# 192 unused bytes per partition among the constants of a transformer layer

## The chip, the cores and the metric

The kernel is one program on 1 core of a Trainium2 chip. The metric is the device time of one execution in microseconds, median of several runs. Every number below is of the kernel before the change.

## The reference

One layer, batch 1, 1024 positions, model width 1024, all in float32:

```python
x = x + 0.5 * swiglu(rms_norm(x, g_ffn1), w1_gate, w1_up, w1_down)      # d_ff 2816
h = rms_norm(x, g_mix);  proj = h @ w_in                                # 10 slices
y_a = dsa_attention(...)             # indexer scores, top 256 keys of each query, 8 heads of 64
y_b = stick_breaking_attention(...)  # 8 heads of 64, strictly causal
x = x + (sigmoid(g_a) * (y_a @ w_o_a) + sigmoid(g_b) * (y_b @ w_o_b)) @ w_out
x = x + 0.5 * swiglu(rms_norm(x, g_ffn2), w2_gate, w2_up, w2_down)
```

## The kernel before

**Numbers in two parts.** TensorE multiplies in the type float32r. To keep the float32 result, each operand is split into a high part and a low part (`halve`, L375 to L379: ScalarE copies the high part, GpSimd or VectorE subtracts it for the low part), and each product is made of three matmuls: high by high, high by low, low by high (`mm3`, L306 to L310, and `times`, L505 to L511). Almost all matmuls are 128 by 128 by 512: 128 columns of a stationary tile, which are loaded into TensorE, and 512 columns of a moving tile, which are streamed past them. A tile of 1024 float32 per partition (4096 bytes) holds the high part in its first half and the low part in its second.

**Stages.** `ffn_in` (L486) makes the gate and up products of a feed-forward network by a scheme with seven products in place of eight for a 2 by 2 block product: eleven rounds over pairs of 128 hidden columns, gate and up in each, seven products of 12 matmuls each per round and side (`products`, L517; the first round, `opening`, L541, is written out by hand and has plain products for the gate). `ffn_out` (L685) makes the down product by the same scheme (L747 to L749). Both are run once for each of the two feed-forward networks: in the trace the first lies at 28 to 674 us, the second at 1525 to 2174 us. Between them stand the projections, both attentions and the output projections; there a class of the kernel (`Weave`) orders the pieces by a written cost model.

**Two sides of the on-chip memory.** Tiles come from pools that are stacked from both ends of a partition's address range: pools without a `side` from the low end, upwards, pools with `side="right"` from the high end, downwards. Constants lie at the low end ahead of all left pools. The right side holds, among others, the pool `outer` (four tiles `w`, two tiles `raw`), the moving operands of `ffn_in` (`t1`, `t2`: 28 tiles, named aB, aT, bB, bT) and the normed input of the projections (`hpool`). The left side holds a ring of five more operand tiles and two more raw tiles, the sums, the outputs of products and most tiles of the attentions.

`ring` (L818) joins both sides, and its order is that of `in_turn` (L312):

```python
op = in_turn((wt, 4), (lambda name: pool.tile([P, 1024], F32R, tag="r", ...), NR))    # NR = 5
raw = in_turn((rawt, 2), (lambda name: pool.tile([P, 1024], F32, tag="raw", ...), 2))
```

`in_turn` hands out the sources alternately as long as both have tiles left: the nine operand tiles come as right, left, right, left, right, left, right, left, left, and again. In `ffn_in` such a tile is the stationary operand of all 12 matmuls of one product, and the moving operand is always on the right. In `ffn_out` both operands are from the ring.

**Two earlier tiles that nothing uses** stand at the two ends: `edgel`, 24 float32 (96 bytes) first among the constants, and `edger`, 8 float32 (32 bytes) first on the right side.

**Addresses.** In the built program the tiles of 4096 and 2048 bytes on the left side start at 256 modulo 512 bytes, those on the right side at 448 modulo 512 bytes. The columns that a matmul reads start at multiples of 512 bytes within a tile (a block of 128 columns is 512 bytes, a half tile 2048), so this remainder is that of each operand too. Exceptions are the identity matrix of the transposes (224 modulo 512) and the query weights wqi and wuq of the indexer and the sparse attention on the right side (192, 448, 64 and 320).

Of the kernel before, what the change touches and what calls it, by code (L numbers as in the profile page):

```python
# [10 lines left out]
F32 = mybir.dt.float32  # L11
# [12 lines left out]
P = 128  # L24
# [221 lines left out]
def trunk(ctx, tc, x, positions, g_ffn1, w1_gate, w1_up, w1_down, g_mix, w_in, g_cq, w_uq_a, w_q_idx,  # L246
          g_q_a, g_k_a, w_uv_a, w_o_a, w_o_b, w_out, g_ffn2, w2_gate, w2_up, w2_down, inv_freq, out):
    nc = tc.nc
    cst = ctx.enter_context(tc.tile_pool(name="cst", bufs=1))
# [21 lines left out]
    cst.tile([P, 24], F32, name="edgel")  # L271
    ident = cst.tile([P, P], F32, name="ident")
    make_identity(nc, ident)
    mhalf = cst.tile([P, H], F32, name="mhalf")
    nc.vector.memset(mhalf, -0.5)

# [2034 lines left out]
```

## Time and profile before

| | |
|---|---|
| median of 3 runs | 2177.04 us (2176.51 to 2177.9) |
| the profiled execution's own time | 2179.75 us |
| its span (first to last instruction) | 2178.0 us |
| TensorE clock granted, mean | 0.999 |
| TensorE matmuls | 10310 |
| VectorE busy | 1542.6 us (71%) |
| ScalarE busy | 1045.4 us (48%) |
| GpSimd busy | 913.9 us (42%) |
| moved to and from HBM | 172 GB/s over the span |

PE is TensorE's matmul row, PEld its weight loads, DVE VectorE, ACT ScalarE, POOL GpSimd, SPq the queue that issues most transfers. A matmul's record ends after the next one has begun, since matmuls are pipelined: what one costs is the distance from its start to the start of the next, not its own length. Tile names are shown without their numbers, the moving operand first and the stationary one second (`pc<-bT,b19S`: bT moves, b19S is loaded).

### The profile page before, as it was taken

To read this page: it belongs to the slowest core of one execution; us is meant where nothing else is said; L and a number is where in the kernel's file an instruction comes from. 1 tells how busy PE (TensorE), PEld (TensorE's weight loads), DVE (VectorE), ACT (ScalarE), POOL (GpSimd) and SP (SyncE) were. 2 spreads that over 40 slices of the span, in tenths; PEclk is the share of its full clock that TensorE was granted. 3 is DMA by queue.
4 is the path that set the end of the run, shared out by engine and by line. 5 is a ranking of instruction groups with operands and counts; after the bars stand their busy time and mean duration, and the time that the engine had idled before them with its cause. 6 is when DMAs were issued, how large, how long until landed. Compare 5 with 4: busy or idle time off the path is not lost. (4 is left out here: it accounts for less than half of the span.)

```text
span 2178.0 us, 30148 instructions
## 1 busy us (share of the span) xinstructions
PE 2149.0 (99%) x10310; PEld 1777.0 (82%) x10310; DVE 1542.6 (71%) x2620; ACT 1045.4 (48%) x1973; POOL 913.9 (42%) x732
## 2 busy tenths in 40 slices
PE   8999999999999999999999999999999999999999
PEld 6788888888879989788888888888788888888887
DVE  7766767678875499898886788754765646577675
ACT  6333343334445358987875565434432232324443
POOL 5654555522345434322211433254564455542233
PEclk9999999999999999999999999999999999999999
DMA  4577767497675242666744534463132323359655
GB/s 146 152 242 212 242 200 230 153 331 240 207 218 161 99 148 88 233 179 178 193 138 156 192 120 171 150 246 131 55 125 92 116 92 108 101 178 330 216 174 184
DMA packets 277578, 377.33 MB, mean 173 GB/s; under 512 B 39840, under 2 KB 165440, under 8 KB 277424
## 3 DMA queue, kind: packets, MB, share of 16 engines
q1 hardware_dynamic: 265392, 337.61, 48.9%
q0 software_dynamic: 12032, 37.79, 4.5%
q8 instruction: 81, 1.33, 0.2%
q14 instruction: 73, 0.60, 0.1%
HBM read 258.38 MB, written 116.95 MB: 172 GB/s over the span
## 5 line engine op out<-in xcount | busy, mean ns | idle before, releaser
L1295 ACT ACTIVATE junka<-u,cand,sig 128x768 bf16<-128x768 f32 (+1 forms) x124 | 134.4, 1084 | 3.8 <-DVE cand L1287 2.3
L1739 DVE TENSOR_TENSOR_SCAN left<-left 128x640 f32<-128x640 f32 (+3 forms) x64 | 87.4, 1382 | 0.3 <-ACT left L1733 0.2
L870 ACT ACTIVATE swh<-swr 128x512 fp32r<-128x512 f32 x48 | 30.2, 630 | 119.2 <-PE pc L510 52.9
L871 DVE TENSOR_TENSOR swr<-swr,swh 128x512 f32<-128x512 f32 x48 | 42.4, 884 | 36.3 <-ACT swh L870 36.1
L651 ACT ACTIVATE b0u<-b0u 128x512 f32<-128x512 f32 x20 | 12.7, 633 | 103.2 <-DVE b0u L531 85.7
L1797 DVE SCALAR_TENSOR_TENSOR pt<-pstT,pt 128x512 fp32r<-128x512 f32 (+1 forms) x96 | 51.7, 552 | 12.4 <-ACT pt L1794 11.9
L1209 POOL DMA_DIRECT2D gd<-evg x32 | 18.6, 580 | 99.2 <-ACT evg L1204 96.8
L1800 DVE TENSOR_TENSOR pt<-pspT,pt 128x512 fp32r<-128x512 f32 x72 | 46.6, 683 | 17.1 <-ACT pt L1794 16.9
L1794 ACT ACTIVATE pt<-pstT 128x512 fp32r<-128x512 f32 (+1 forms) x96 | 46.2, 492 | 24.1 <-PE pstT L1854 22.0
L1794 ACT ACTIVATE pt<-pspT 128x512 fp32r<-128x512 f32 x72 | 39.5, 596 | 33.3 <-PE pspT L2012 33.0
L1921 DVE CUSTOM_DVE_ANT_0 e<-psL,bias 128x512 f32<-128x512 f32 (+3 forms) x96 | 49.8, 551 | 7.5 <-PE psL L1958 7.4
L1933 ACT ACTIVATE e<-e,nm 128x768 f32<-128x768 f32 (+7 forms) x64 | 49.3, 775 | 10.5 <-DVE nm L1928 10.3
L748 PE MATMUL p<-aT,aS 128*128 128x512 f32 x132 | 52.4, 397 | 1.9 <-DVE aT L378 1.9
L1652 DVE SCALAR_TENSOR_TENSOR u<-relu,WI,u 128x512 f32<-128x512 f32 (+1 forms) x70 | 49.3, 723 | 3.7 <-ACT relu L1645 2.7
L749 PE MATMUL p<-aT,aS 128*128 128x512 f32 x132 | 51.8, 397 | 0.0
L748 PE MATMUL p<-bT,bS 128*128 128x512 f32 x132 | 51.6, 391 | 0.0
L749 PE MATMUL p<-bT,bS 128*128 128x512 f32 x132 | 51.0, 391 | 0.0
L1645 ACT ACTIVATE relu<-psdot 128x512 f32<-128x512 f32 (+1 forms) x80 | 39.8, 519 | 22.6 <-DVE u L1652 13.4
L747 PE MATMUL p<-bT,bS 128*128 128x512 f32 x132 | 47.4, 392 | 0.0
L747 PE MATMUL p<-aT,aS 128*128 128x512 f32 x132 | 45.9, 397 | 0.7 <-ACT aT L377 0.7
L1854 PE MATMUL pstT<-ident,left 128*128 128x128 f32 x288 | 45.9, 273 | 0.0
L1733 ACT ACTIVATE left<-psz 128x512 f32<-128x512 f32 (+2 forms) x96 | 44.0, 501 | 2.5 <-PE psz L1762 2.1
(3051 smaller groups left out, 8218.9 us busy)
## 6 DMA issues: line engine op xcount, KB each, us to landing
aw<-in_w_down_dram SPq DMA_DIRECT2D x33, 512.0 KB, 5.0
bw<-in_w_down_dram SPq DMA_DIRECT2D x33, 512.0 KB, 4.7
swr<-in_w_in_dram SPq DMA_DIRECT2D x48, 256.0 KB, 5.4
a0r<-in_w_gate_dram SPq DMA_DIRECT2D x22, 512.0 KB, 7.5
a1r<-in_w_up_dram SPq DMA_DIRECT2D x22, 512.0 KB, 6.9
b0r<-in_w_gate_dram SPq DMA_DIRECT2D x22, 512.0 KB, 3.9
b1r<-in_w_up_dram SPq DMA_DIRECT2D x22, 512.0 KB, 3.7
x<-in_x_dram SPq DMA_DIRECT2D x16, 512.0 KB, 5.9
```

Source lines behind the costliest of these rows:

```text
L747: nc.tensor.matmul(ps[q][m], S[:, h], T[:, HI], start=p == 0, stop=False)
L748: nc.tensor.matmul(ps[q][m], S[:, h], T[:, LO], start=False, stop=False)
L749: nc.tensor.matmul(ps[q][m], S[:, l], T[:, HI], start=False, stop=p == last)
L1295: nc.scalar.activation(junks[1][:, 0:(i + 1) * P], score[i], AF.Sign, scale=sig[:, b:b + 1], bias=cand.bitcast(F32)[:, b:b + 1], accum_out ...
L1652: nc.vector.scalar_tensor_tensor(ac, r, wv, ac, op0=ALU.mult, op1=ALU.add)
L1739: nc.vector.tensor_tensor_scan(back, back, back, 1.0, op0=ALU.mult, op1=ALU.bypass)
L1794: nc.scalar.activation(pt[:, off:512], tp[:, off:512], AF.Copy, bias=-less)
L1797: nc.vector.scalar_tensor_tensor(pt[:, 512 + off:1024], tp[:, off:512], -less, f32(pt[:, off:512]), op0=ALU.add, op1=ALU.subtract)
L1800: nc.vector.tensor_sub(pt[:, 512 + off:1024], tp[:, off:512], f32(pt[:, off:512]))
L1854: nc.tensor.transpose(tp[:, q * P:(q + 1) * P], A[n + q][:, j * P:(j + 1) * P], ident)
L1921: nc.vector.tensor_tensor_reduce(e[:, c], lp[:, 0:n_], bias[:, c], 1.0, LOW, op0=ALU.add, op1=ALU.max, accum_out=m)
L1933: nc.scalar.activation(e[:, 0:nk], e[:, 0:nk], AF.Exp, bias=nm_, accum_out=ssum)
```

## The change

A tile of 48 float32, which nothing writes or reads, is allocated among the constants behind the identity matrix:

```diff
     cst.tile([P, 24], F32, name="edgel")
     ident = cst.tile([P, P], F32, name="ident")
     make_identity(nc, ident)
+
+    cst.tile([P, 48], F32, name="pad")
     mhalf = cst.tile([P, H], F32, name="mhalf")
```

The built program has the same instructions in the same order on every engine (9849 shown rows on TensorE, 2465 on VectorE, 1645 on ScalarE, 703 on GpSimd, 954 on the transfer queue, each the same as before but for line numbers and the running numbers in tile names). All that moves is addresses: every tile on the left side that lies behind the identity matrix starts 192 bytes higher, so that the left tiles named above go from 256 to 448 modulo 512 bytes, where the right ones are. The right side, the identity matrix and `edgel` stay where they were.

## The prediction

> **What bounds the kernel now.** I read the page first: the shares of the engines, the clock, and the chain that ended last.
>
> ```profile
> span 2178.0 us, 30148 instructions
> PE 2149.0 (99%) x10310; PEld 1777.0 (82%) x10310; DVE 1542.6 (71%) x2620; ACT 1045.4 (48%) x1973; POOL 913.9 (42%) x732
> PEclk9999999999999999999999999999999999999999
> PE 34%; DVE 0%; ACT 0%; POOL 0%; issue 0%; ACTq 0%; DVEq 0%
> ```
>
> TensorE is busy from end to end at the full clock, and the chain names hardly anything else. So the time is the sum of the distances from the start of one matmul to the start of the next. No instruction moves; only addresses do. The question is whether that distance depends on addresses.
>
> Next I read TensorE's timeline, start by start, first where both operands of all matmuls are on the right side (projection of the gates, weights wg, input mhi and mlo), with the count of that stretch from the windows view:
>
> ```profile
> core 0: us, PE busy (x) PEld busy (x) DVE busy (x) ACT busy (x) POOL busy (x), PEclk, DMA share, GB/s
> 1133.00:1178.00 45.00, 45.00 (x200) 37.28 (x199) 23.57 (x86) 29.56 (x51) 7.50 (x14) 1.00 0.49 168
> ...
> 1132.76 0.39 PE L308 MATMUL psf<-mhi,wg0h 128*128 128x512 f32 x1
> 1132.98 0.39 PE L309 MATMUL psf<-mlo,wg0h 128*128 128x512 f32 x1
> 1133.21 0.39 PE L310 MATMUL psf<-mhi,wg0l 128*128 128x512 f32 x1
> ...
> 1177.86 0.39 PE L309 MATMUL psf<-mlo,wg4h 128*128 128x512 f32 x1
> ```
>
> Of the 200 matmuls two began ahead of the stretch; 198 begin in it, and 44.65 us over 197 distances is 226.7 ns each. This is the floor in what follows. Now two products of `ffn_in` in a row, 12 matmuls each. By the ring's order the stationary S2 of this batch (product pb) is on the right and the S3 (pc) on the left; the moving operand is on the right in both.
>
> ```profile
> 1905.91 0.39 PE L508 MATMUL pb<-bT,b19S 128*128 128x512 f32 x1
> ...
> 1907.30 0.39 PE L508 MATMUL pb<-bT,b19S 128*128 128x512 f32 x1
> ...
> 1908.66 0.40 PE L508 MATMUL pc<-bT,b19S 128*128 128x512 f32 x1
> 1908.90 0.39 PE L509 MATMUL pc<-bT,b19S 128*128 128x512 f32 x1
> 1909.13 0.40 PE L510 MATMUL pc<-bT,b19S 128*128 128x512 f32 x1
> ...
> 1911.46 0.39 PE L508 MATMUL pd<-bT,b19S 128*128 128x512 f32 x1
> ```
>
> The mixed product takes 2.80 us, 233 ns a matmul, from its first pair on (0.24, 0.23). The right-right one takes 2.75 us: its first six take 1.39 us (232 ns), its last six 1.36 us (227 ns). So after a mixed product the next one needs about six matmuls until it is at the floor. Does it need them after any product? Two right-right products in a row, in the opening round:
>
> ```profile
> 1536.01 0.39 PE L508 MATMUL pg<-bB,b00A 128*128 128x512 f32 x1
> ...
> 1538.76 0.39 PE L508 MATMUL pa<-bB,b10A 128*128 128x512 f32 x1
> ...
> 1541.26 0.39 PE L510 MATMUL pa<-bB,b10A 128*128 128x512 f32 x1
> ```
>
> The first follows a mixed one and takes 2.75 us; the second has 11 distances in 2.50 us, 227 ns, with no slow start. The slow start is thus left over from the mixed product, and where all are alike it goes as well.
>
> **Side or offset?** Mixed pairs differ both in side and in offset (256 against 448), and the change alters only the offset. The query projections tell the two apart, since all their operands are on the right side. The stationary cqh and cql start at 448 modulo 512; the moving wqi tiles at 192 and 448 (256 or 0 apart), the wuq tiles at 64 and 320 (128 or 384 apart). Each of these runs is six matmuls:
>
> ```profile
> 755.80 0.39 PE L308 MATMUL psq<-wqih,cqh 128*128 128x512 f32 x1
> ...
> 757.16 0.39 PE L1675 MATMUL psdot<-kih,qsi 128*128 128x512 f32 x1
> ...
> 887.84 0.40 PE L308 MATMUL psq<-wuqh,cqh 128*128 128x512 f32 x1
> ...
> 889.23 0.39 PE L308 MATMUL psf<-mhi,wqk10322h 128*128 128x512 f32 x1
> ```
>
> 1.36 us with offsets 256 or 0 apart, the floor; 1.39 us with 128 or 384 apart, 232 ns, on one side. So it is the offset, and what counts seems to be whether the two agree modulo 256. Mixed pairs are 192 or 320 apart now, and 0 after the change.
>
> [...]
>
> **The change part by part.** The pad itself is never written: no instruction, no transfer, 0 us. It moves left tiles alone, so left-left and right-right pairs keep their difference. Then, by stretches in which TensorE never waits and nearly all matmuls are of 512 columns:
>
> ```profile
> 65.00:628.00 563.00, 563.00 (x2441) 458.17 (x2440) 396.81 (x524) 215.63 (x385) 265.14 (x171) 1.00 0.71 221
> 1575.00:2165.00 590.00, 590.00 (x2558) 480.15 (x2558) 375.57 (x468) 203.55 (x361) 263.99 (x182) 1.00 0.47 157
> 1430.00:1499.00 69.00, 69.00 (x298) 55.43 (x297) 33.85 (x39) 24.68 (x34) 39.47 (x19) 1.00 0.68 237
> ...
> 640.00:1430.00 790.00, 781.99 (x4355) 665.80 (x4354) 623.48 (x1422) 512.01 (x1043) 269.35 (x301) 1.00 0.50 160
> ```
>
> A stretch also counts the matmuls still running at its start: 0.39 over 0.23 us, 1.7 of them. At the floor:
> - 65 to 628 us (both halves of the first feed-forward network): 2439.3 x 0.22665 = 552.9 us, 10.1 less than now.
> - 1575 to 2165 us (the second): 2556.3 x 0.22665 = 579.4 us, 10.6 less.
> - 1430 to 1499 us (output projection; its M and weight tiles are on both sides): 296.3 x 0.22665 = 67.2 us, 1.8 less.
>
> A count over `ffn_in` alone checks this. Each call has 15 products in its opening round and 20 batches of 7, 155 in all; 5 of the 9 ring tiles are on the left, so 86 are mixed and 69 not. Twice 86 x (2.80 - 2.72) plus twice 69 x (2.75 - 2.72) is 17.9 us; the 140 products of the batches have 16.2 of it, which leaves 4.5 of the 20.7 us for `ffn_out`, where both operands alternate.
>
> - 640 to 1430 us (attentions). Mixed pairs are few (the value products, and changes from a left-left to a right-right piece); transposes and short matmuls stand between, and the gate projections are at the floor already. Bounds: 0, and the feed-forward share (20.7 of 1153 us, 1.8%) of 790 us, 14 us. TensorE waits 8 us here, so part of any gain turns into waits. I take 1.5, near the lower end, because of the 1133 us row.
> - What is left is the opening rounds and the end, bounded by 0 and 1.8% of about 166 us, 3 us; I take 0.5, since these waits follow:
>
> ```profile
> PE p L748 <- DVE aT L378: 1.9, 1, 1.9
> ...
> PE pa L510 <- POOL a01A L378: 1.5, 1, 1.5
> PE pa L510 <- POOL b01A L378: 1.5, 1, 1.5
> ```
>
> Those on POOL end the opening rounds, where VectorE and GpSimd make operands behind TensorE: what TensorE saves there it waits. The one on DVE, at 633 us, ends the `ffn_out` in which VectorE has the rope tables to make besides; between 0 and what TensorE saves in this `ffn_out` (half of 4.5 us) is lost again; I take 0.8.
>
> Costed at nothing: the 560 transposes from left tiles, whose difference to the identity goes from 32 to 224 modulo 256. Tiles on the right have 224 already, and run alike (by on the left, x on the right: both 109 ns apart, once 0.27 us for the last record is taken off):
>
> ```profile
> 1498.92 3.66 PE L432 MATMUL pst<-ident,by 128*128 128x128 f32 x32
> ...
> 1541.49 1.69 PE L432 MATMUL pst<-ident,x 128*128 128x128 f32 x14
> ```
>
> Sum: 10.1 + 10.6 + 1.8 + 1.5 + 0.5 - 0.8 = 23.7 us. The profiled execution took 2179.75 us by its own clock, which gives 2156.0 us; the median of the runs is 2.7 us lower, 2177.04, which gives 2153.3 us. I take 2153.
>
> **Rivals.**
> - The slow start comes back at every product, because something other than the mixed one before it sets it off. Then a mixed product falls only to 2.75 us: 172 x 0.05 = 8.6 of the 17.9 us, and in proportion 11.4 of 23.7 us in all: 2165.6 us. The 2.50 us row speaks against it.
> - Nothing happens, because 448 against 448 across the sides is not like it within a side: 2177 us. The query rows speak against it, though with few matmuls. [...]
> - Slower, through transfers into left tiles. They start at a multiple of 256 bytes now and 192 past one afterwards. Right tiles have that start already, and weights go to both in turn:
>
> ```profile
> L480 SPq DMA_DIRECT2D b0r<-in_w_gate_dram x4: 384/384/386, 1611.8 to 1652.7; - x4
> L377 ACT ACTIVATE b03A<-b0r x3: 615/616/633, 1628.5 to 1647.0; 128x512 fp32r<-128x512 f32 x3
> ...
> DMA to landing us min/median/max: 3.9/4.4/4.8
> ```
>
> A load issued at 1611.8 has landed by 1616.6 and is first read at 1628.5, 11.9 us later. If left loads were late by 1 us beyond this, each of the 44 pairs of weight loads in `ffn_in` would stall TensorE by 1 us: 44 - 23.7 = 20 us slower, 2197 us. It decides only from 12 us of extra landing time on; the whole spread of four loads, left and right, is 0.9 us. [...]
> - VectorE or GpSimd becomes the bound in `ffn_in`, and a third or more of the gain turns into waits: 2163 to 2170 us. VectorE is busy 397 of 563 us (70%) and GpSimd 265, which leaves room for a TensorE that is 2% quicker.
>
> **Chances.** Forecast (2147 to 2163 us) 0.80; slow start comes back 0.08; part of the gain waits 0.04; nothing 0.06; slower 0.02. The low end of the range takes 6 us more from the attentions and 1 from the openings, whose upper bounds are 14 and 3; the high end takes those two as 0 and lets a third of the 22.5 us go. 0.2% (4.4 us) is about what a measurement of this kernel can tell from no change; faster by more has 0.80 + 0.08 + 0.04 = 0.92, the same 0.05, slower 0.03.
>
> **What would show it.** Right: in the profile after, all products of `ffn_in` take 2.72 us, with equal distances from the first to the last; the two feed-forward stretches hold as many matmuls in 11 and 10 us less; the gate projections stay at 226.7 ns. Wrong: mixed products still alternate (nothing), 2.75 us for each (slow start), or new waits on DVE, POOL or transfers in the rounds.

## The result and the profile after

| | before | after |
|---|---|---|
| median, same chip | 2176.78 us (2176.06 to 2177.9, 4 runs) | 2152.64 us (2150.32 to 2153.47, 4 runs) |
| the profiled execution's own time | 2179.75 us | 2150.32 us |
| its span | 2178.0 us | 2148.6 us |

The ratio of after to before is 0.9887 (95% interval 0.987 to 0.9904): 24.1 us less between the medians, where 23.7 us were forecast. The two profiled executions are 29.4 us apart, because that of before was 2.7 us slower than the first median and that of after is 2.3 us faster than its own; that has to be kept in mind when stretches are compared.

The head of the page after, and its chain of work that ended last:

```profile
span 2148.6 us, 30148 instructions
PE 2122.4 (99%) x10310; PEld 1776.4 (83%) x10310; DVE 1537.6 (72%) x2620; ACT 1044.2 (49%) x1973; POOL 920.3 (43%) x732
PEclk9999999999999999999999999999999999999999
...
PE 32%; DVE 1%; ACT 1%; issue 0%; DMA 0%; POOL 0%; ACTq 0%; DVEq 0%; POOLq 0%
```

The same instructions, the same full clock, TensorE is still the bound, and its busy time is 26.6 us shorter. The other engines' busy times moved by 6.4 us or less. Line numbers of after are two higher than those of before (L508 is L510).

TensorE's timeline after, for the products that the prediction showed (S2 and S3 of the same batch, and the start of the two that follow):

```profile
1880.53 0.39 PE L510 MATMUL pb<-bT,b19S 128*128 128x512 f32 x1
...
1883.25 0.39 PE L510 MATMUL pc<-bT,b19S 128*128 128x512 f32 x1
1883.48 0.39 PE L511 MATMUL pc<-bT,b19S 128*128 128x512 f32 x1
1883.71 0.39 PE L512 MATMUL pc<-bT,b19S 128*128 128x512 f32 x1
...
1885.97 0.39 PE L510 MATMUL pd<-bT,b19S 128*128 128x512 f32 x1
...
1888.69 0.39 PE L510 MATMUL pa<-bB,b19A 128*128 128x512 f32 x1
```

Each product takes 2.72 us: pb was 2.75, pc 2.80. The same stretches of the program as in the prediction, cut in the trace of after so that they hold the same numbers of matmuls (2441, 2558, 298 and 4355):

```profile
63.77:617.41 553.64, 553.30 (x2441) 457.95 (x2440) 400.52 (x526) 216.36 (x388) 267.06 (x172) 1.00 0.73 226
1556.36:2135.79 579.43, 579.43 (x2558) 479.76 (x2558) 373.82 (x468) 203.35 (x361) 267.03 (x182) 1.00 0.48 160
1414.07:1482.26 68.19, 67.69 (x298) 55.40 (x297) 33.67 (x39) 24.67 (x34) 38.83 (x19) 1.00 0.69 239
625.78:1414.07 788.29, 781.05 (x4355) 666.54 (x4354) 622.47 (x1425) 512.14 (x1043) 268.54 (x301) 1.00 0.51 160
```

The first feed-forward network's stretch falls from 563.00 to 553.64 us, the second's from 590.00 to 579.43, the output projection's from 69.00 to 68.19, and the attentions' from 790.00 to 788.29. That is 22.45 of the 29.4 us. The rest lies between them: the start (65.00 to 63.77, 1.2 us), the piece from the first network to the projections (12.00 to 8.37, 3.6 us), the second network's opening (76.00 to 74.10, 1.9 us) and the end (0.2 us). The 3.6 us are taken up below: they are not the change's.

A second way of counting, used for all runs below: each start of a 512-column matmul in the trace is paired with the addresses that its operands have in the built program, and the distances to the next start are averaged (those above 260 ns are left out). In `ffn_in` before, 2056 mixed matmuls average 233.2 ns and 1654 agreeing ones 228.9 ns; after, all 3713 average 226.7 ns. What all of them take above 226.67 ns falls from 17.3 to 0.2 us in `ffn_in`, from 5.8 to 0.2 us in `ffn_out` and from 7.9 to 5.2 us elsewhere.

### The profile page after: what moved, and what is told of

The parts are those of the page before. It is cut to its first block, busy times and chain, and to the rows that moved or that the text cites. A ratio compares the mean times of both kernels' runs of the same rounds, so it can differ in the third digit from the quotient of the medians.

```text
span 2148.6 us, 30148 instructions
## 1 busy us (share of the span) xinstructions
PE 2122.4 (99%) x10310; PEld 1776.4 (83%) x10310; DVE 1537.6 (72%) x2620; ACT 1044.2 (49%) x1973; POOL 920.3 (43%) x732
```

## The experiments

In all of them the right tiles start at 448 modulo 512 unless the text says otherwise. "Difference" is the moving operand's address less the stationary one's, modulo 256. Every run has its own runs of the kernel before on the same chip; ratios are to those.

| run | left, right modulo 512 | difference of mixed pairs in `ffn_in` | mixed / agreeing there, ns | median us (range) | ratio (95%) |
|---|---|---|---|---|---|
| before | 256, 448 | 192 | 233.2 / 228.9 | 2176.78 (2176.06 to 2177.9) | 1 |
| after | 448, 448 | 0 | all 226.7 | 2152.64 (2150.32 to 2153.47) | 0.9887 (0.987 to 0.9904) |
| left192 | 192, 448 | 0 (256 apart) | all 226.7 | 2151.04 (2150.94 to 2152.74) | 0.9879 (0.9862 to 0.9895) |
| right256 | 256, 256 | 0 | all 226.7 | 2152.27 (2151.91 to 2153.55) | 0.9883 (0.9868 to 0.9898) |
| both416 | 416, 416 | 0 | all 226.7 | 2152.99 (2150.41 to 2155.33) | 0.9884 (0.9866 to 0.9902) |
| ident | 448, 448; identity 192 | 0 | all 226.7 | 2152.02 (2151.72 to 2152.99) | 0.9879 (0.9865 to 0.9894) |
| left320 | 320, 448 | 128 | 232.9 / 229.2 | 2177.2 (2175.3 to 2178.02) | 0.9992 (0.9983 to 1.0001) |
| left416 | 416, 448 | 32 | 232.8 / 227.4 | 2175.94 (2173.86 to 2178.95) | 0.9992 (0.9983 to 1.0001) |
| oneodd | 192, 448; one ring tile 192 bytes higher | 64, one product in nine | 229.0 / 226.7 | 2156.21 (2153.87 to 2156.68) | 0.9896 (0.9881 to 0.9911) |
| odd64 | 192, 448; one ring tile 64 bytes higher | 192, one product in nine | 233.2 / 227.0 | 2158.83 (2157.64 to 2161.07) | 0.9908 (0.9894 to 0.9921) |
| left384 | 384, 448 | 64 | 229.0 / 226.7 | 2164.56 (2163.36 to 2166.61) | 0.9933 (0.9921 to 0.9946) |

**left192: without the pad, the first constant smaller.** The left tiles move down instead of up and do not share the right side's remainder modulo 512, only modulo 256:

```diff
-    cst.tile([P, 24], F32, name="edgel")
+    cst.tile([P, 8], F32, name="edgel")
```

> No pad; the tile edgel is 64 bytes shorter, so that the left tiles start at 192 modulo 512, 256 away from the right ones at 448. Theory (operands must agree modulo 256): like the changed kernel, 2153 us (2150 to 2156), equal distances of 226.7 ns in all products. Rival (they must agree modulo 512): like the kernel before, about 2177 us, mixed products of 2.80 us.

TensorE's timeline, three products of the second network in a row:

```profile
1575.54 0.39 PE L508 MATMUL pb<-bT,b11S 128*128 128x512 f32 x1
...
1578.26 0.39 PE L508 MATMUL pc<-bT,b11S 128*128 128x512 f32 x1
...
1580.98 0.39 PE L508 MATMUL pd<-bT,b11S 128*128 128x512 f32 x1
```

2.72 us each and 2151.04 us in all: 256 bytes apart is as good as 0 apart. The change gives both sides one offset modulo 512, which is more than is needed.

**left320: the pad a third as long.** The left tiles move by 64 bytes, 128 apart from the right:

```diff
+    cst.tile([P, 16], F32, name="pad")
```

> A pad of 64 bytes in place of 192: left tiles at 320 modulo 512, 128 away from the right ones. Theory (agree modulo 256): about 2177 us, since 128 is as bad as 64; mixed products of about 2.80 us. Rival (agree modulo 128, or the price falls with the distance): 2153 us, or between the two.

```profile
1904.79 0.40 PE L510 MATMUL pc<-bT,b19S 128*128 128x512 f32 x1
...
1907.59 0.40 PE L510 MATMUL pd<-bT,b19S 128*128 128x512 f32 x1
...
1910.34 0.40 PE L510 MATMUL pa<-bB,b19A 128*128 128x512 f32 x1
...
1913.14 0.40 PE L510 MATMUL pc<-bT,b19A 128*128 128x512 f32 x1
```

Mixed 2.80, agreeing behind it 2.75, mixed 2.80 us, as before. A pad alone brings nothing, and agreeing modulo 128 is not enough.

**left416: the pad 160 bytes.** The left tiles lie 32 bytes below the right ones modulo 512:

```diff
+    cst.tile([P, 40], F32, name="pad")
```

> A pad of 160 bytes: left tiles at 416 modulo 512, 32 away from the right ones. Theory (any disagreement modulo 256 costs the same): about 2177 us. Rival (only multiples of 64 count, so that 32 away still falls into the same piece): 2153 us. Second rival (being no multiple of 64 costs by itself): above 2177 us.

```profile
1903.97 0.39 PE L510 MATMUL pc<-bT,b19S 128*128 128x512 f32 x1
...
1906.77 0.39 PE L510 MATMUL pd<-bT,b19S 128*128 128x512 f32 x1
...
1908.13 0.39 PE L510 MATMUL pd<-bT,b19S 128*128 128x512 f32 x1
...
1909.49 0.39 PE L510 MATMUL pa<-bB,b19A 128*128 128x512 f32 x1
```

Nothing is gained at 32 bytes apart: the mixed product takes 2.80 us, 232.8 ns a matmul. The agreeing one behind it has no slow start here: its first six matmuls take 1.36 us, and so do its last six. (The agreeing ones still average 227.4 ns, because the step from such a product to the next mixed one takes 235 ns.) But `ffn_out` is slower (7.2 us above the floor in place of 5.8), and the time is that of before within the interval.

**right256: no pad, the right side moved.** The left tiles stay where they were, the right ones come to 256:

```diff
-    ...tile_pool(name="edge", bufs=1, side="right")).tile([P, 8], F32, name="edger")
+    ...tile_pool(name="edge", bufs=1, side="right")).tile([P, 56], F32, name="edger")
```

> No pad; edger is 192 bytes longer, so that the right tiles come down to 256 modulo 512, where the left ones are. Theory (only the difference counts): 2153 us (2150 to 2156). Rival (448 itself is the good place, or moving the left tiles did it): 2177 us or slower.

2152.27 us: the gain does not come from where the left tiles lie, nor from the constants behind the identity matrix, which have not moved in this run.

**both416: both sides moved to the same new place,** neither of the two before (`edger` 16 floats, `pad` 40):

> Left and right tiles agree at 416 modulo 512 (edger 32 bytes longer, pad 160 bytes), no multiple of 64 or 128. Theory (only the difference counts): 2153 us. Rival (a start that is no multiple of 64 costs by itself): slower than 2153 by some us, with distances above 226.7 ns everywhere.

2152.99 us, all products at 226.7 ns. So none of the three remainders that both sides have had in common (448, 256 and 416) is good or bad by itself: all products take 226.7 ns a matmul at each of them, and 448 against 256, 320, 384 or 416 does not give it.

**ident: the identity matrix moved too,** so that the transposes' operands agree modulo 256 as well (`edgel` 16 floats, `pad` 56):

> As the changed kernel, but the identity matrix is moved too: edgel 32 bytes shorter, the pad 32 bytes longer, so that the identity lies at 192 modulo 512, 256 away from the left and right tiles (it was 32 away modulo 256). The 856 transposes have the identity as moving operand. Theory A (the rule on offsets holds for transposes as well, and the slow starts that are left in the attentions come from the unlike transposes): the 109 ns between transposes or the slow starts after them fall; 2147 to 2150 us. Rival B (transposes have a bound of their own, and a slow start follows any short matmul): 2152 to 2153 us, no change against the changed kernel.

The two groups of transposes that the prediction costed at nothing, in this run:

```profile
1482.76 3.65 PE L434 MATMUL pst<-ident,by 128*128 128x128 f32 x32
...
1524.65 3.66 PE L434 MATMUL pst<-ident,x 128*128 128x128 f32 x32
```

32 transposes take 3.65 and 3.66 us; before, the group of by took 3.66 us. Over all transposes the distance is 108.9 to 109.1 ns in every run. So their pace does not follow the offset of the identity matrix, and this run's time is that of after.

**oneodd: all agree but one tile of the ring.** From left192, one of the nine ring tiles is put 192 bytes higher, between two small unused tiles:

```diff
+        r4 = lambda name: pool.tile([P, 1024], F32R, tag="r", name=name, bufs=NR - 1)
+        def r1(name):                     # 48 unused floats ahead of this tile, 16 behind it
+            t = pool.tile([P, 1024], F32R, tag="rx", name=name, bufs=1)
...
-        op = in_turn((wt, 4), (lambda name: pool.tile(..., bufs=NR), NR))
+        op = in_turn(*[(f, 1) for f in [wt, r4] * 4 + [r1]])
```

> As left192 (all operands agree modulo 256), but one of the nine ring tiles of the feed-forward networks stands 192 bytes higher, between two unused tiles of 192 and 64 bytes. 34 products of ffn_in are mixed (172 before), and 420 matmuls of ffn_out (588 before). Theory (a mixed product costs 0.08 us, and the next one 0.03 for its slow start): 34 x 0.11 = 3.7 us in ffn_in and some 3.8 in ffn_out, about 7.5 us over left192: 2158.5 us (2157 to 2160); in the timeline one product in nine at 2.80, the one behind it at 2.75, the others at 2.72. Rival (no slow start behind a single mixed product): 2156 us, all but one in nine at 2.72. Second rival (one odd tile upsets the pace of all): 2165 us or more.

```profile
1899.10 0.39 PE L509 MATMUL pa<-bB,b010A 128*128 128x512 f32 x1
...
1901.84 0.39 PE L509 MATMUL pb<-bT,b010S 128*128 128x512 f32 x1
...
1904.56 0.39 PE L509 MATMUL pc<-bT,b010S 128*128 128x512 f32 x1
```

By the medians it is dearer than left192 by 5.2 us, but those are of two chips; than ident, on its own chip, it is dearer by 4.2 us. Both are less than expected. The rows show why: the odd product (pa) takes 2.74 us in place of 2.80, and the one behind it starts at full pace, 2.72 us. Two readings were open. The odd product may be cheap because it stands alone among agreeing ones; or because its difference is 64, where that of before was 192. The two runs that follow part them.

**odd64: the odd tile 64 bytes higher instead of 192,** so that the same products at the same places have a difference of 192 (48 and 16 floats changed round):

> As the run with one odd ring tile in nine, but the odd tile starts 64 bytes above the other right tiles in place of 192. So the products of ffn_in with the odd tile as stationary operand have the moving operand 192 above it modulo 256, as the mixed products of the kernel before; their number and places are those of the run with one odd tile. Theory 1 (the sign of the difference counts): the odd matmuls of ffn_in take 233 ns and the product behind each has the slow start, so the excess of ffn_in is about 3.6 us in place of 1.1 us, and the time some 2.5 us above that of the run with one odd tile: 2158.6 us (2157 to 2160.5). Theory 2 (standing alone makes them cheap): 229.0 ns and 226.7 ns as there, excess of ffn_in 1.1 us, 2156.2 us (2154 to 2157).

```profile
1904.54 0.40 PE L509 MATMUL pa<-bB,b010A 128*128 128x512 f32 x1
...
1907.34 0.39 PE L509 MATMUL pb<-bT,b010S 128*128 128x512 f32 x1
...
1910.09 0.39 PE L509 MATMUL pc<-bT,b010S 128*128 128x512 f32 x1
```

The same lone product now takes 2.80 us and its follower 2.75 us, exactly as before. `ffn_in` lies 3.7 us above the floor (3.6 expected, 1.1 in oneodd), and the median is 2158.83 us where 2158.6 was expected.

**left384: 64 everywhere.** After, with a pad of 32 floats:

> All left tiles start at 384 modulo 512 bytes (the pad is 32 floats instead of 48), the right ones stay at 448. So the mixed pairs of ffn_in have the moving operand 64 above the stationary one modulo 256, at the same places of the program where the kernel before has 192. In the run with one odd ring tile the odd products of ffn_in had 64 as well; their matmuls took 229.0 ns in place of the 233.2 ns of before, and no slow start followed. Theory 1, the sign of the difference counts (64 is cheaper than 192): mixed matmuls of ffn_in take about 229 ns, and the agreeing ones behind them 226.7 ns, so the excess of ffn_in over 226.67 ns falls from 17.3 us to about 5 us; ffn_out has both signs and keeps about 4.2 of its 5.8 us; in all some 10 us more than with all agreeing: 2161 us (2158 to 2164). Theory 2, the odd products were cheap because they stood alone, eight agreeing tiles between them: here every second product is mixed again, as before, so mixed matmuls take 233 ns, a slow start follows, and the time is 2177 us (2174 to 2179).

```profile
1894.24 0.39 PE L510 MATMUL pc<-bT,b19S 128*128 128x512 f32 x1
...
1896.99 0.39 PE L510 MATMUL pd<-bT,b19S 128*128 128x512 f32 x1
...
1899.71 0.39 PE L510 MATMUL pa<-bB,b19A 128*128 128x512 f32 x1
...
1902.45 0.39 PE L510 MATMUL pc<-bT,b19A 128*128 128x512 f32 x1
```

Mixed 2.75 and 2.74 us, agreeing 2.72 us with no slow start, though every second product is mixed. `ffn_in` is 4.85 us above the floor (5 expected). So at 64 bytes apart the direction of the difference counts (229.0 ns for 64, 233.2 for 192), and standing alone does not. The time, 2164.56 us, is 0.6 us above the expected range (the two of its five executions with a granted clock of 1.000 took 2163.36 and 2163.74 us, inside it). What was reckoned too small is `ffn_out`: either operand may be the left one there, so it has both 64 and 192, and it lies 6.0 us above the floor, not 4.2. Agreeing products hold 2.95 us of that; most of them do not even follow a mixed one, as the next section shows.

## Why the prediction was right, point by point

**The floor, and that all products reach it.** Right. Of the 310 products of `ffn_in`, 301 take 2.72 us after (of the other nine, five hold a distance of more than 300 ns and two stand behind such a product), and its matmuls average 226.7 ns, the floor read from the gate projections. Those keep their pace: their 45 us hold the same 200 matmuls in both traces.

```profile
1117.37:1162.37 45.00, 45.00 (x200) 37.27 (x199) 23.53 (x87) 29.61 (x52) 7.59 (x14) 1.00 0.49 168
```

**The slow start is left over from the mixed product.** Right for `ffn_in`: no mixed ones, no slow start. The rival in which it comes back at each product (2165.6 us) falls with the rows of after. What the prediction did not have is, first, that in `ffn_in` it follows some differences only: 192 and 128 bring it (agreeing products behind mixed ones take 2.75 us before and in left320), 64 and 32 do not (2.72 us in left384 and left416). Second, a mixed product is not needed for it. In `ffn_out` left-left and right-right products also stand directly behind one another. Three of them in the second network, left-left, right-right, left-left by the ring's order, the first behind another left-left one; before, and then left384:

```profile
2016.56 0.61 PE L747 MATMUL p<-bT,bS 128*128 128x512 f32 x2
...
2019.28 0.39 PE L747 MATMUL p<-bT,bA 128*128 128x512 f32 x1
...
2022.01 0.39 PE L747 MATMUL p<-bT,bS 128*128 128x512 f32 x1
...
2024.77 0.39 PE L747 MATMUL p<-bB,bA 128*128 128x512 f32 x1
```

```profile
2001.24 0.61 PE L749 MATMUL p<-bT,bS 128*128 128x512 f32 x2
...
2003.96 0.39 PE L749 MATMUL p<-bT,bA 128*128 128x512 f32 x1
...
2006.72 0.39 PE L749 MATMUL p<-bT,bS 128*128 128x512 f32 x1
...
2009.45 0.39 PE L749 MATMUL p<-bB,bA 128*128 128x512 f32 x1
```

Left-left behind left-left takes 2.72 us in both. Before, right-right behind left-left takes 2.73 and left-left behind right-right 2.76 us (227.7 and 230.2 ns a matmul on the mean of all such products); in left384 the two change places. That fits the difference between the moving operand of the product that ends and the stationary one of the product that begins, which is 64 and 192 before and 192 and 64 in left384; that this pair is the cause is not shown. After, all of them average 226.7 ns.

**Offset, not side.** Right. Left192, right256 and both416 keep the two sides and only make the offsets agree, and all three have the whole gain; left320 and left416 move the left tiles as well, without agreement, and have none of it. The rival "nothing" (2177 us) falls with them. With the instructions unchanged the three that agree are 23 to 26 us below the two that do not.

**Agreement modulo 256.** Right, drawn from six matmuls each of wqi and wuq, and now shown by left192 (256 apart, good) and left320 (128 apart, bad). The wuq products, 128 or 384 apart on one side, are not touched by the change and have not moved; TensorE's timeline after, from a run of six to the row behind it:

```profile
872.66 0.40 PE L310 MATMUL psq<-wuqh,cqh 128*128 128x512 f32 x1
...
874.05 0.39 PE L310 MATMUL psf<-mhi,wqk10322h 128*128 128x512 f32 x1
```

1.39 us, as before.

**The terms of the sum.**

| stretch | forecast us | measured between the profiled executions, us |
|---|---|---|
| first feed-forward network | -10.1 | -9.4 |
| second feed-forward network | -10.6 | -10.6 |
| output projection | -1.8 | -0.8 |
| attentions | -1.5 | -1.7 |
| openings and end | -0.5 | -3.3 |
| wait on DVE at 633 us | +0.8 | +0.7, against left320 (below) |

The two large terms and the attentions came out as worked; the first network lacks 0.7 us nearly all of it by a new wait for VectorE, taken up below. The output projection was put at the floor, and nearly all its matmuls are there (distances up to 260 ns average 227.1 ns). What keeps its stretch 1.0 us above that is four longer gaps; three small ones stand in before too, and the longest by far is a new wait on GpSimd, the last row below, of 0.5 us; left416, which has no gain, has 0.4 us of it too. The waits on TensorE's queue, after:

```profile
PE p L750 <- DVE aT L380: 1.2, 2, 0.9
...
PE pa L512 <- POOL b01A L380: 0.9, 1, 0.9
PE pa L512 <- POOL a01A L380: 0.8, 1, 0.8
...
PE psout L311 <- POOL wout010l L299: 0.5, 1, 0.5
```

The openings were under-sized by a wrong step. I had said that what TensorE saves ahead of the two waits on POOL it waits there. Both waits got shorter instead, 1.5 to 0.9 and 0.8 us, so the openings kept what their matmuls gained and 1.3 us more. GpSimd's work there is not independent of TensorE: in the opening, ScalarE copies the results of TensorE's transposes and products and GpSimd continues from these copies, so a quicker TensorE can bring it forward too; that is read from the kernel and not tested. That the waits go with the pace of the products is shown by the other runs (1.5 us in left320 and left416, 0.8 in left192, right256, ident, both416 and the cheaper left384); why they shrink rather than stay is not settled.

The wait on DVE took gain back about as forecast, but the trace of before cannot show it: 1.9 us before, 1.2 after. In that one profiled execution TensorE waited longer at this place than in the other runs with mixed products, and right behind the wait the granted clock was halved for 3.41 us:

```profile
633.85:637.26 3.41, 3.41 (x10) 2.64 (x9) 3.41 (x3) 1.79 (x3) 2.41 (x2) 0.50 0.69 214
```

Left320 and left416 have mixed products and the full clock there. Both have 0.5 us of this wait; the row of left320:

```profile
PE p L750 <- DVE aT L380: 0.5, 1, 0.5
```

After has 0.7 us more than that (0.3 at 499 us, inside the first network's stretch, and 0.9 at 620 us), where 0.8 was forecast. That forecast started from the disturbed 1.9 us, so its closeness is partly luck. Left192, right256, both416 and ident wait 1.7 to 1.9 us for VectorE in `ffn_out`. So the 3.6 us that the piece from the first network to the projections fell by are no gain: its 32 distances from 628.15 us on take 12.06 us before, 8.15 in left320, 8.18 in left416 and 8.49 after. Of the 3.9 us between before and left320 about 1.6 are the halved clock (nine distances of 276 to 427 ns, which make 3.65 us where 2.04 would be the floor), and the rest is mostly the longer waits, whose reason no run shows.

Without this piece the two executions differ by 25.8 us, which goes with the 24.1 us between the medians. That the forecast's 23.7 us comes so close is partly luck: the openings' 2.8 us too little stands against the output projection's 1.0 and the first network's 0.7 us too much.

**Slower through transfers.** Did not happen. The profile page's median from issue to landing is the same row before and after, where left raw tiles went from 256 to 448 modulo 512:

```profile
b0r<-in_w_gate_dram SPq DMA_DIRECT2D x22, 512.0 KB, 3.9
```

TensorE has no wait on a transfer in the rounds of either `ffn_in`. The page does not part left and right loads, so it cannot show whether the left ones alone take a little longer; if they do, it is hidden.

**Part of the gain lost in waits, or another engine the bound.** A small part: 0.7 us on VectorE in `ffn_out`, which the forecast had, and 0.5 us on GpSimd in the output projection. No other engine became the bound: in the first network's stretch VectorE is busy for 400.52 of 553.64 us (72%), and the new wait for it there is 0.3 us.

**No version beats this one.** Left192, ident and right256 have the same time within their intervals, and left192 does it with fewer bytes. What is still above the floor, 5.2 us outside the feed-forward networks, lies in the attentions and what is woven in with them, much of it behind short matmuls and gaps (4.4 us within six matmuls of one), and was the same in every run with agreeing operands (5.2 to 5.4 us). It was not taken apart further.

## What to carry to other kernels

Where TensorE streams float32r matmuls back to back and is the bound, compare the byte address of moving and stationary operand: here 226.7 ns a matmul if the two agree modulo 256, up to 233 ns if not, and 192 unused bytes at one end of the memory settled it. Look for it by the starts in the timeline, product by product: two paces for the same shape were the sign here (2.80 and 2.75 us a product before, 2.72 after). Then test it by moving the other side, or by making the same remainder elsewhere, since a pad changes every address behind it at once.

## What the runs showed of the hardware that was not expected

- At 64 bytes apart the direction of the difference counts. Moving less stationary address of 64 modulo 256 costs 229.0 ns a matmul in `ffn_in` and leaves no slow start; 192 costs 233.2 ns and leaves six slow matmuls; 128 costs 232.9 ns and leaves about as many; 32 costs 232.8 ns and leaves none. In `ffn_out` before, both directions stand side by side: 230.7 ns for 64, 233.4 for 192. What mechanism lies behind it stays open: the runs only show the dependence, and other differences were not tried.
- In `ffn_out` a slow start also follows a change between left-left and right-right products, with no mixed one between them (230.2 ns a matmul at a difference of 192 across the change, 227.7 at 64).
- Transposes (128 columns) have the same 109 ns in every run, with the identity 32 or 224 from the stationary tile modulo 256 (before) as with 0 (ident).
- In the profiled execution of before the granted clock was 0.50 for 3.41 us at 634 us, which cost about 1.6 us. Those of odd64 and left384 have the same mean granted clock as it, 0.999; the eight others have 1.000. What sets it off stays open.
